# First sweep of a bidirectional recurrent mixer: four passes of 512 tokens, or two of 1024

## The chip, the cores and the metric

The kernel runs on one core of one Trainium2 chip. The metric is device time of one execution in microseconds. Before the change it was 2407.32 us, the median of three runs (2403.57 to 2407.87).

TensorE is called PE in the profile, VectorE DVE, ScalarE ACT, GpSimd POOL and SyncE SP; PEld is TensorE's loading of weights. All transfers are issued from SP's queue.

## The reference

One layer: a bidirectional RG-LRU mixer, then a SwiGLU feed-forward, each with RMS norm, a conditioning shift and scale, and a gated residual. There are T = 2048 latent tokens and 256 context tokens of width D = 1024; the recurrent width is R = 1280, that is NB = 10 columns of 128; the feed-forward is 2816 wide. Cut to what matters:

```python
u = short_conv(h @ w_rec)                       # 4 taps along the tokens, context and latent apart
for d in range(2):                              # forward, backward
    r, i = sigmoid(u @ gate_w[d] + gate_b[d])   # block diagonal, one 128 x 128 block per column n
    log_a = -8 * r * softplus(-lam[d])
    a = exp(log_a); b = sqrt(-expm1(2 * log_a)) * i * u
    h_ctx = scan(a_ctx, b_ctx, 0)               # context first
    h_lat[d] = scan(a_lat, b_lat, h_ctx[-1])    # its last state starts the latent scan
x = x + g1 * ((h_lat[0] + h_lat[1]) * gelu(h @ w_gate)) @ w_out
x = x + g2 * swiglu(norm(x))
```

Products keep nearly full precision: each operand is split into a high part (a cast on ScalarE) and a low part (a subtraction on VectorE), and each product is three matmuls, high x high, high x low, low x high (`mm3`, lines 124 to 126).

## The kernel before, in words

The work is tiled in chunks of C = 512 tokens. **Sweep 1** (`sweep1`, line 561) goes through the four chunks in order of time, the context joined to chunk 0. The tables `ORDER` (line 33) give each pass its order of jobs, for the ten columns n: r(n) is the projection with w_rec and the conv (`rec_unit`, `conv`), g(n) the projection with w_gate (`gate_unit`), z(n) the products of the two directions' gates (`z_unit`). Both weights are read from DRAM and split again in every pass (`unit`, `parts`, lines 99 and 102), and so is gate_w.

The forward scan runs in each pass (`a_tables`, `a_unit`): exp and tanh on ScalarE, square root, then two products and a scan on VectorE (lines 539 to 542), for groups of two to five columns at a time. The backward scan can only start at the end of time. So for chunks 0 to 2 the backward gates go to DRAM (`d_ab`), with the forward states (`d_hf`) and the gate projection (`d_g`); chunk 3, the last pass, scans both directions on chip. Its sum goes to DRAM for six columns (`d_rec`), and `gelus`, `rg_last` take its GELUs and products.

Chunk 2 is brought back while pass 3 runs (`back_some`, `back_units`, `back_load`, `back`): gates, forward states and gate projection are loaded, its tables, backward scan and GELU product run, and `d_rg` is written. Since a pass's conv lacks the two tokens to its right, chunks overlap by two (`halo`, `edge`).

**Sweep 2** (`sweep2`, line 940) takes chunks 3 and 2 together: the output projection of each (`w_out`, tile ps_wo, five pairs of columns read from `d_rg`), the second norm, sums of parts (`combos`), the feed-forward's first product (`up`) with the backward part of chunks 1 and 0 beside it, their output projection, and the second product (`down`).

What the planner decides: the order of instructions on each engine comes from priorities and a simulated timeline; `behind` adds an order within a queue, and `table` keeps all functions of ScalarE that need a table in the order of the program.

Buffers in PSUM: seven single banks under one tag (`bank`, line 129) and one for small sums. In SBUF: rings by tag; `raw` (4) and `op` (6) for weights and other split operands; two rings for the normed activations, so that those of the next chunk can be made while the last ones are read (`norm1_apply`).

Of the kernel before, what the change touches and what calls it, by code (L numbers as in the profile page):

```python
# [12 lines left out]
P = 128  # L13
D = 1024
# [7 lines left out]
NC_ = T // C  # L22
TC = 256
EPS = 1e-6
# [4 lines left out]
RAWS = 4  # L29


KIND = dict(r="rec", g="gate", z="z")
ORDER = (
# [17 lines left out]
class Trunk:  # L51
# [10 lines left out]
    def __init__(self, tc, io):  # L62
        self.tc, self.nc, self.io = tc, tc.nc, io
        self.last_table = self.turn = self.after = None
# [3 lines left out]
    def table(self, ins):  # L68

        if self.last_table is not None:  # L70
            self.behind(ins, self.last_table)
        self.last_table = ins.ins.name
        return ins

    def in_turn(self, ins):

        if self.turn is not None:
            if self.turn:
                self.behind(ins, self.turn)
            self.turn = ins.ins.name  # L80
        return ins
# [10 lines left out]
    def parts(self, raw, name, n=2 * C, eng_h=None, turn=False):  # L92

        nc = self.nc
        t = self.wp.tile([P, 2, n], F32R, tag="op", name=f"op_{name}", bufs=OPS)
        if eng_h == "v":
            nc.vector.tensor_copy(t[:, 0, :], raw)
        else:
            ins = nc.scalar.copy(t[:, 0, :], raw)  # L99
            if turn:  # L100
                self.in_turn(ins)
        nc.vector.tensor_tensor(out=t[:, 1, :], in0=raw, in1=t[:, 0, :].bitcast(F32), op=ALU.subtract)  # L102
        return t
# [88 lines left out]
    def constants_rest(self):  # L192
# [14 lines left out]
        self.edge = cp.tile([P, NB, 3, 2], F32, name="edge")  # L207
# [28 lines left out]
    def mod_first(self):  # L236
# [10 lines left out]
        st = self.te.tile([P, KD, P], F32R, tag="xtok", name="mod_st", bufs=1)  # L247
# [11 lines left out]
    def mod_quarter(self, q):  # L259
        nc, st, sel = self.nc, self.mod_st, self.sel  # L260
        ps = self.bank(f"ps_mod{q}")
        for k in range(KD):
            raw = self.tp.tile([P, C], F32, tag="i", name=f"raw_modf{q}_{k}", bufs=self.ni)
            self.last_mod = nc.sync.dma_start(raw, self.io["mod_f"][q, k]).ins.name
            tags, bufs = (("a", "a"), self.na) if k % 3 == 0 else (("uh", "ul"), self.nu)
            h, l = (self.te.tile([P, C], F32R, tag=tag, name=f"w{s}_modf{q}_{k}", bufs=bufs)
                    for s, tag in zip("hl", tags))
            nc.scalar.copy(h, raw)
            nc.vector.tensor_tensor(out=l, in0=raw, in1=h.bitcast(F32), op=ALU.subtract)
            for w in (h, l):  # L270
                nc.tensor.matmul(ps, st[:, k, :], w, start=(k == 0 and w is h), stop=(k == KD - 1 and w is l))
        rows = self.tp.tile([P, C], F32, tag="g", name=f"mod_rows{q}", bufs=2)
        nc.scalar.copy(rows, ps)
        pc = self.pp.tile([P, C], F32, tag="st", name=f"ps_modc{q}", bufs=1)[:, :8].rearrange("p (i s) -> p i s", s=2)
# [37 lines left out]
    def norm1_load(self, seg, j):  # L312

        t0 = seg * C + j * P
        xt = self.te.tile([P, D], F32, tag="xtok", name=f"xtok{seg}_{j}", bufs=1)
        self.behind(self.nc.sync.dma_start(xt, self.io["x"][t0 : t0 + P]), self.last_raw)
        return xt

    def norm1_stats(self, seg, j, xt):

        nc = self.nc
        n = C // P
        if j == 0:
            self.ss = self.sp.tile([P, n], F32, tag=f"ss{n}", name=f"ss{seg}", bufs=2)
        self.behind(nc.scalar.activation(xt, xt, AF.Square, accum_out=self.ss[:, j : j + 1]), self.last_X)
        return self.rstd_of(self.ss, f"rstd{seg}") if j == n - 1 else None

    def first_loads(self, seg):

        nc = self.nc  # L330
        n = TC if seg < 0 else C
        src = self.io["ctx_t"] if seg < 0 else self.io["x_t"][seg]
        xs = []
        w = C // n
        for k in range(0, KD, w):
            if seg < 0:
                t = self.te.tile([P, w, n], F32, tag="u", name=f"xc{k}", bufs=self.nu)
            else:
                t = self.tp.tile([P, w, n], F32, tag="r", name=f"x0_{k}", bufs=self.nr)
            nc.sync.dma_start(t, src[:, k : k + w, :])  # L340
            xs += [t[:, j, :] for j in range(w)]
        return xs

    def first_stats(self, xs):

        nc = self.nc
        n0 = TC // P
        ps = self.bank("ss_first", n0 + C // P)
        for s, n, c0 in ((-1, TC, 0), (0, C, n0)):
            acc = self.te.tile([P, C], F32, tag="xr", name=f"acc{s}", bufs=3)[:, :n]  # L350
            for k in range(KD):
                sq = acc
                if k:
                    sq = self.tp.tile([P, C], F32, tag="g", name=f"sq{s}_{k}", bufs=2)[:, :n]
                nc.scalar.activation(sq, xs[s][k], AF.Square)
                if k:
                    nc.vector.tensor_tensor(out=acc, in0=acc, in1=sq, op=ALU.add)
            for j in range(n // P):
                nc.tensor.matmul(ps[:, c0 + j : c0 + j + 1], acc[:, j * P : (j + 1) * P], self.ones[:, :1],
                                 start=(c0 == j == 0), stop=(c0 > 0 and j == C // P - 1), skip_group_check=True)  # L360
        y = self.rstd_of(ps, "rstd_first")
        return {-1: y[:, :n0], 0: y[:, n0:]}

    def first_scale(self, xs, bc, after=None):
        for x in xs:
            ins = self.nc.vector.tensor_tensor(out=x, in0=x, in1=bc, op=ALU.mult)
            if after:
                self.behind(ins, after)

    def norm1_apply(self, seg, bc, xs=None, ks=range(KD)):  # L370
        nc = self.nc
        s = 1 if seg < 0 else 0
        n = TC if seg < 0 else C
        out = []
        for k in ks:
            if xs is None:
                xr = self.te.tile([P, C], F32, tag="xr", name=f"xr{seg}_{k}", bufs=3)
                dma = nc.sync.dma_start(xr, self.io["x_t"][seg][:, k, :])
                if self.after:
                    self.behind(dma, self.after)  # L380
            else:
                xr = xs[k]
            a, b = self.A[:, k, s : s + 1], self.B[:, k, s : s + 1]
            if xs is None:
                nc.vector.scalar_tensor_tensor(out=xr, in0=xr, scalar=a, in1=bc, op0=ALU.mult, op1=ALU.mult)
            else:
                nc.vector.tensor_scalar(out=xr, in0=xr, scalar1=a, scalar2=b, op0=ALU.mult, op1=ALU.add)
            if seg < 0:
                hl = self.hp.tile([P, 2, TC], F32R, tag="hx0", name=f"hc{k}", bufs=KD)
                h, l = hl[:, 0, :], hl[:, 1, :]  # L390
            else:
                ring = ("hx1", "hx0", "hx1", "hx1")[seg] if k < KD // 2 else ("hx1", "hx1", "hx0", "hx1")[seg]
                bufs = KD if ring == "hx0" else 2 * KD
                h = self.hp.tile([P, C], F32R, tag=ring, name=f"hh{seg}_{k}", bufs=bufs)
                l = self.hp.tile([P, C], F32R, tag=ring, name=f"hl{seg}_{k}", bufs=bufs)
            if xs is None:
                nc.scalar.activation(h, xr, AF.Identity, bias=b, scale=1.0)  # L397
                nc.vector.scalar_tensor_tensor(  # L398
                    out=l, in0=xr, scalar=b, in1=h.bitcast(F32), op0=ALU.add, op1=ALU.subtract)
            else:  # L400
                nc.scalar.copy(h, xr)
                nc.vector.tensor_tensor(out=l, in0=xr, in1=h.bitcast(F32), op=ALU.subtract)
            out.append((h, l))
        return out

    def slot(self, tag, seg, n, dt=F32):

        if seg >= 0:
# [644 lines left out]
```

## Time and profile before

| | us |
|---|---|
| median of three runs | 2407.32 |
| the profiled execution | 2408.78 |
| its span, first to last instruction | 2407.0 |
| TensorE busy | 2226.5 |
| VectorE busy | 1609.9 |
| ScalarE busy | 1268.0 |

Busy times are of one engine over the whole span. TensorE's clock, as granted, was 0.964 of full speed in the mean. The four passes of sweep 1 begin at 57, 248.4, 397.6 and 544 us, the output projection of chunks 3 and 2 at 746 and the feed-forward's share of the span some 180 us after that.

How to read the rows: a timeline row is start, duration, engine, line, operation and out<-in, with idle time before it in brackets. A group row is line, engine, operation, shapes and count, then busy time and mean nanoseconds of one, then the engine's idle time before them and what ended it. A wait row says which instruction waited for which other one: sum, times, longest.

### The profile page before, as it was taken

To read this page: it belongs to the slowest core of one execution; us is meant where nothing else is said; L and a number is where in the kernel's file an instruction comes from. 1 tells how busy PE (TensorE), PEld (TensorE's weight loads), DVE (VectorE), ACT (ScalarE), POOL (GpSimd) and SP (SyncE) were. 2 spreads that over 40 slices of the span, in tenths; PEclk is the share of its full clock that TensorE was granted. 3 is DMA by queue.
4 is the path that set the end of the run, shared out by engine and by line. 5 is a ranking of instruction groups with operands and counts; after the bars stand their busy time and mean duration, and the time that the engine had idled before them with its cause. 6 is when DMAs were issued, how large, how long until landed. Compare 5 with 4: busy or idle time off the path is not lost.

```text
span 2407.0 us, 27419 instructions
## 1 busy us (share of the span) xinstructions
PE 2226.5 (93%) x9810; PEld 1828.6 (76%) x9810; DVE 1609.9 (67%) x2446; ACT 1268.0 (53%) x1799; POOL 1.6 (0%) x7
## 2 busy tenths in 40 slices
PE   6999899997866785999999999999999999999999
PEld 4888687875754663778777888888888888888887
DVE  8888878887787558666766656874555555544443
ACT  6588776576897533564646444543333333333332
POOL 0000000000000000000000000000000000000000
PEclk8999999998987897999999999999999999999999
DMA  8444567765436764334443478786632222235664
GB/s 282 158 147 171 185 201 245 231 201 166 137 127 215 265 222 131 109 130 165 132 159 128 154 245 277 241 283 229 208 101 79 93 87 84 79 120 199 230 219 151
DMA packets 163721, 420.24 MB, mean 175 GB/s; under 512 B 19200, under 2 KB 26880, under 8 KB 163584
## 3 DMA queue, kind: packets, MB, share of 16 engines
q1 hardware_dynamic: 163584, 418.49, 52.2%
q8 instruction: 76, 1.25, 0.2%
q14 instruction: 61, 0.50, 0.1%
HBM read 333.51 MB, written 84.90 MB: 174 GB/s over the span
## 4 chain that ended last, share of the span: by engine, by line
PE 62%; DVE 14%; ACT 13%; DMA 6%; issue 4%; SPq 0%; DVEq 0%; ACTq 0%
PE ps_dn L124 7%; PE ps_dn L126 7%; PE ps_dn L125 7%; PE ps_be L124 6%; PE ps_be L125 6%; PE ps_be L126 6%; ACT L90 3%; PE ps_ep L126 3%; PE ps_ep L125 3%; PE ps_ep L124 3%; DMA raw_mod<-in_mod_t 2%; PE ps_wo L124 2%; PE ps_wo L125 2%; PE ps_wo L126 2%; ACT r L90 2%
## 5 line engine op out<-in xcount | busy, mean ns | idle before, releaser
L126 PE MATMUL ps_dn<-op_xd,op_wd 128*128 128x512 f32 x704 | 274.7, 390 | 0.0
L125 PE MATMUL ps_dn<-op_xd,op_wd 128*128 128x512 f32 x704 | 273.9, 389 | 0.0
L124 PE MATMUL ps_dn<-op_xd,op_wd 128*128 128x512 f32 x704 | 269.1, 389 | 0.0
L102 DVE TENSOR_TENSOR op_wd<-raw_wd,op_wd 128x1024 fp32r<-128x1024 f32 x88 | 107.7, 1224 | 197.1 <-ACT op_wd L99 197.1
L99 ACT CAST op_wd<-raw_wd 128x1024 fp32r<-128x1024 f32 x88 | 92.7, 1053 | 259.2 <-PE ps_dn L126 210.5
L887 DVE TENSOR_TENSOR s<-ps_ep,s 128x512 f32<-128x512 f32 x88 | 60.7, 690 | 150.9 <-ACT s L912 111.8
L124 PE MATMUL ps_wo<-op_xo,op_wo 128*128 128x512 f32 x320 | 125.3, 408 | 33.6 <-ACT op_xo L99 33.6
L126 PEld LDWEIGHTS ps_dn<-op_xd,op_wd 128*128 128x128 f32 x704 | 132.1, 188 | 28.2 <-issue 0.5
L124 PEld LDWEIGHTS ps_dn<-op_xd,op_wd 128*128 128x128 f32 x704 | 132.1, 188 | 27.6 <-issue 0.5
L125 PEld LDWEIGHTS ps_dn<-op_xd,op_wd 128*128 128x128 f32 x704 | 132.1, 188 | 27.5
L124 PE MATMUL ps_be<-T,op_b 128*128 128x512 f32 x352 | 139.3, 396 | 9.4 <-ACT s L912 9.4
L124 PE MATMUL ps_ep<-T,op_s 128*128 128x512 f32 x352 | 137.3, 391 | 9.3 <-ACT T L827 9.3
L126 PE MATMUL ps_be<-T,op_b 128*128 128x512 f32 x352 | 138.2, 393 | 0.0
L125 PE MATMUL ps_be<-T,op_b 128*128 128x512 f32 x352 | 138.2, 393 | 0.0
L126 PE MATMUL ps_ep<-T,op_s 128*128 128x512 f32 x352 | 137.4, 390 | 0.0
L125 PE MATMUL ps_ep<-T,op_s 128*128 128x512 f32 x352 | 137.4, 390 | 0.0
L912 ACT COPY s<-ps_be 128x512 f32<-128x512 f32 x44 | 25.6, 583 | 205.9 <-PE ps_be L126 205.9
L125 PE MATMUL ps_rec<-hl,op_rec 128*128 128x512 f32 x320 | 127.1, 398 | 4.8 <-DVE hl L398 4.8
L90 ACT ACT_TABLE_LOAD x96 | 123.2, 1283 | 12.5 <-DMA g<-d_g 6.2
L125 PE MATMUL ps_wo<-op_xo,op_wo 128*128 128x512 f32 x320 | 127.8, 400 | 0.9 <-DVE op_xo L102 0.9
L124 PE MATMUL ps_rec<-hh,op_rec 128*128 128x512 f32 x320 | 127.8, 401 | 0.8 <-ACT hh L397 0.5
L126 PE MATMUL ps_wo<-op_xo,op_wo 128*128 128x512 f32 x320 | 127.2, 397 | 0.0
(506 smaller groups left out, 5695.1 us busy)
## 6 DMA issues: line engine op xcount, KB each, us to landing
raw_wd<-in_down SPq DMA_DIRECT2D x88, 512.0 KB, 3.7
raw_xd<-d_act SPq DMA_DIRECT2D x88, 512.0 KB, 4.7
raw_ga<-in_gu SPq DMA_DIRECT2D x44, 512.0 KB, 4.0
raw_gb<-in_gu SPq DMA_DIRECT2D x44, 512.0 KB, 4.2
d_act<-s SPq DMA_DIRECT2D x88, 256.0 KB, 3.5
raw_rec<-in_w_rec SPq DMA_DIRECT2D x40, 512.0 KB, 4.4
raw_gate<-in_w_gate SPq DMA_DIRECT2D x40, 512.0 KB, 3.8
raw_wo<-in_w_out SPq DMA_DIRECT2D x40, 512.0 KB, 4.6
```

Source lines behind the costliest of these rows:

```text
L90: return self.table(self.nc.scalar.activation(out, in_, func, bias=bias, scale=scale))
L99: ins = nc.scalar.copy(t[:, 0, :], raw)
L102: nc.vector.tensor_tensor(out=t[:, 1, :], in0=raw, in1=t[:, 0, :].bitcast(F32), op=ALU.subtract)
L124: ins = mm(ps, w[0], x[0], start=first, stop=False, skip_group_check=shared)
L125: mm(ps, w[0], x[1], start=False, stop=False, skip_group_check=shared)
L126: mm(ps, w[1], x[0], start=False, stop=last, skip_group_check=shared)
L887: v.tensor_tensor(out=t, in0=ps, in1=t, op=ALU.add)
L912: nc.scalar.copy(s3, be)
```

## The change

Sweep 1 has two passes of S = 1024 tokens. Each weight is read and split once per pass. The context is joined to the first pass and gets its own tiles, with two tokens of the second pair appended to it, so that the conv at the end of the first pair has its right neighbour's projection and the overlap of chunks goes.

- PSUM in sweep 1 is three pairs of banks (`pair`) and two single ones (`bank`); in sweep 2 eight single ones. ScalarE and VectorE ops on latent tokens are 1024 wide.
- Each column's scan comes right after its z (`scan_unit`); groups of columns go. In the first pass the forward scan and both context scans run, and `d_g`, `d_hf` and `d_ab` hold the first pair alone.
- In the second pass both directions are scanned on chip. The GELU comes straight from PSUM, and `rg_unit` adds, multiplies and writes `d_rg` for chunks 2 and 3. `d_rec`, `gelus`, `rg_last`, `back_some` and the backward part of chunk 2 go.
- The normed activations of the second pair (`norm1_apply`) go into the same ring of eight as the first pair's. Its sums of squares come from 1024-wide rows in the first pass (`norm1_stats`).
- At the start the sums of squares are made by one-column matmuls for each k, the modulation weights come in transfers of 512 KB through the rings `raw` and `op`, and the second half of the first pair is normed after the first half and the context.
- Modulation rows (`mod_rest`) come two at a time.

```diff
 ORDER = (
-    "r0 r1 g0 r2 z0 g1 r3 z1 r4 z2 g2 r5 g3 z3 r6 z4 r7 z5 g4 r8 g5 z6 g6 r9 z7 g7 g8 g9 z8 z9",
...
+    "r0 r1 z0 g0 r2 z1 g1 r3 z2 g2 r4 z3 g3 r5 z4 g4 r6 z5 g5 r7 z6 g6 r8 z7 g7 r9 g8 g9 z8 z9",
+    "r0 r1 z0 g0 r2 z1 g1 r3 z2 g2 r4 z3 g3 r5 z4 g4 r6 z5 g5 r7 z6 g6 r8 z7 g7 r9 z8 z9 g8 g9",
 )
...
     def bank(self, name, n=C):
-        t = self.pp.tile([P, C], F32, tag="ps", name=name, bufs=7)
+        tag, bufs = ("p1", 2) if self.first else ("ps", 8)
+        t = self.pp.tile([P, C], F32, tag=tag, name=name, bufs=bufs)
...
+    def hx_tiles(self, s):
+        ts = [self.hp.tile([P, 2, S], F32R, tag="hx", name=f"hx{s}_{k}", bufs=KD) for k in range(KD)]
+        return [(t[:, 0, :], t[:, 1, :]) for t in ts]
...
+    def pair(self, name):
+        return self.pp.tile([P, S], F32, tag="p2", name=name, bufs=3)
...
+    def rec_unit(self, s, n, w):
+
+        ps = self.pair(f"ps_rec{s}_{n}")
+        if s == 0:
+            self.project(s, ps, w, (0,))
+            psc = self.bank(f"ps_recc_{n}")[:, :TX]
+            self.project(s, psc, w, ctx=self.hc)
+            self.project(s, ps, w, (1,))
+        else:
+            psc = None
+            self.project(s, ps, w)
...
+            r, i = self.wtile(f"r{s}_{n}_{d}"), self.wtile(f"i{s}_{n}_{d}")
+            for q, dst in ((1, i), (0, r)):
+                ps = self.pair(f"ps_z{s}_{n}_{d}{q}")
+                for h in range(2):
+                    self.mm3(ps[:, h * C : (h + 1) * C], wg[q], part(U["p"], h * C, (h + 1) * C), True, True)
+                self.act(dst, ps, AF.Sigmoid, bias=bias(q))
...
+        for d, a, r, i, st, w in todo:
+            self.act(a, r, AF.Exp, scale=self.c_a[:, d, n : n + 1])
+            self.act(r, r, AF.Tanh, scale=self.c_t[:, d, n : n + 1])
+        for d, a, r, i, st, w in todo:
+            self.act(r, r, AF.Sqrt)
...
+    def rg_unit(self, n):
+
+        nc = self.nc
+        (f, b), g = self.rec.pop(n), self.gel.pop(n)
+        nc.vector.tensor_tensor(out=f, in0=f, in1=b, op=ALU.add)
+        nc.vector.tensor_tensor(out=f, in0=f, in1=g, op=ALU.mult)
+        for q in range(2):
+            nc.sync.dma_start(self.d_rg[2 + q][n // 2][:, n % 2, :], f[:, q * C : (q + 1) * C])
```

## Rows read from the trace of the kernel before

**Rows 1.** The profile page: the span, busy time of each engine.

```profile
span 2407.0 us, 27419 instructions
...
PE 2226.5 (93%) x9810; PEld 1828.6 (76%) x9810; DVE 1609.9 (67%) x2446; ACT 1268.0 (53%) x1799; POOL 1.6 (0%) x7
```

**Rows 2.** Windows: stretch, length, busy (x) of PE, PEld, DVE, ACT, POOL, PEclk, DMA.

```profile
0.00:57.00 57.00, 35.92 (x116) 24.81 (x117) 49.25 (x108) 38.65 (x68) 1.59 (x7) 0.89 0.82 284
57.00:248.40 191.40, 184.80 (x962) 156.78 (x963) 163.66 (x362) 145.47 (x261) 0.00 (x0) 0.99 0.49 163
248.40:397.60 149.20, 141.24 (x605) 114.98 (x604) 122.70 (x225) 101.67 (x160) 0.00 (x0) 0.97 0.65 207
397.60:544.00 146.40, 141.35 (x603) 113.55 (x602) 116.68 (x201) 99.62 (x151) 0.00 (x0) 0.99 0.69 218
544.00:746.00 202.00, 153.77 (x722) 130.47 (x720) 160.06 (x279) 165.61 (x269) 0.00 (x0) 0.86 0.47 152
746.00:913.30 167.30, 123.33 (x491) 98.47 (x490) 105.05 (x155) 77.83 (x92) 0.00 (x0) 0.86 0.67 227
```

**Rows 3.** Timeline of PE: start, duration; matmuls of 512 and of 256 columns.

```profile
600.44 0.39 PE L125 MATMUL ps_rec<-hl,op_rec 128*128 128x512 f32 x1
600.66 0.39 PE L126 MATMUL ps_rec<-hh,op_rec 128*128 128x512 f32 x1
...
604.80 0.28 PE L124 MATMUL ps_z_0t<-uh,op_gw 128*128 128x256 f32 x1
604.91 0.28 PE L125 MATMUL ps_z_0t<-ul,op_gw 128*128 128x256 f32 x1
```

**Rows 4.** Waits of PE from 544 to 746: sum, times, longest.

```profile
PE ps_z L124 <- ACT i L90: 22.8, 3, 13.3
PE ps_z L124 <- ACT uh L461: 10.0, 1, 10.0
PE ps_z L124 <- ACT g L90: 5.7, 1, 5.7
PE ps_z_1t L124 <- DVE u L454: 3.7, 1, 3.7
PE ps_z_0t L124 <- ACT i L90: 3.4, 1, 3.4
```

**Rows 5.** Waits of PE from 746 to 913.3.

```profile
PE ps_wo L124 <- ACT op_xo L99: 33.6, 3, 13.9
```

**Rows 6.** Windows of tile ps_wo alone, its second pair of chunks.

```profile
1380.00:1502.00 122.00, 109.22 (x480) 90.09 (x480) 10.21 (x15) 1.00 0.77 260
```

**Rows 7.** Instruction groups of ACT, 57 to 746: busy, mean ns, idle before.

```profile
L90 ACT ACT_TABLE_LOAD x46 | 59.0, 1283 | 1.7 <-DMA bg<-d_g 0.9
L99 ACT CAST op_gate<-raw_gate 128x1024 fp32r<-128x1024 f32 x38 | 39.9, 1054 | 9.8 <-PE ps_gate L126 3.1 <-DMA raw_gate<-in_w_gate 3.1 <-PE ps_rec L126 2.0
...
L90 ACT ACTIVATE i<-ps_z,c_gate_b 128x512 f32<-128x512 f32 x40 | 27.9, 699 | 1.8 <-PE ps_z L126 1.8
```

**Rows 8.** Instruction groups of DVE, 57 to 746.

```profile
L454 DVE SCALAR_TENSOR_TENSOR u<-ps_rec,c_conv_w,u 128x512 f32<-128x512 f32 x120 | 88.6, 744 | 20.1 <-ACT u L451 19.4
L102 DVE TENSOR_TENSOR op_gate<-raw_gate,op_gate 128x1024 fp32r<-128x1024 f32 x40 | 48.7, 1217 | 4.6 <-ACT op_gate L99 4.5
...
L542 DVE TENSOR_TENSOR_SCAN i<-a,state,r 128x512 f32<-128x512 f32 x20 | 25.3, 1274 | 0.0
...
L542 DVE TENSOR_TENSOR_SCAN ic<-ac,rc 128x256 f32<-128x256 f32 x20 | 13.4, 680 | 0.0
```

**Rows 9.** Timeline of PE: the sums of squares at the start.

```profile
17.20 1.70 PE L359 MATMUL ss_first<-ones,acc 128*128 128x1 f32 x8
```

**Rows 10.** Timeline of PE right after a wait in pass 3.

```profile
549.40 0.63 PE L126 MATMUL ps_rec<-hh,op_rec 128*128 128x512 f32 x1
...
549.83 0.63 PE L124 MATMUL ps_rec<-hh,op_rec 128*128 128x512 f32 x1
```

**Rows 11.** DMA issues on the page: KB each, us to landing.

```profile
raw_wo<-in_w_out SPq DMA_DIRECT2D x40, 512.0 KB, 4.6
```

More of the change, by code (lines that the diff above doesn't have):

```diff
@@ L29 @@
 RAWS = 4
-KIND = dict(r="rec", g="gate", z="z")
+WS = 9
+CW = 11
 ORDER = (
[4 rows of a table removed]
+    "r0 r1 z0 g0 r2 z1 g1 r3 z2 g2 r4 z3 g3 r5 z4 g4 r6 z5 g5 r7 z6 g6 r8 z7 g7 r9 g8 g9 z8 z9",
+    "r0 r1 z0 g0 r2 z1 g1 r3 z2 g2 r4 z3 g3 r5 z4 g4 r6 z5 g5 r7 z6 g6 r8 z7 g7 r9 z8 z9 g8 g9",
 )
@@ L63, in __init__ @@
         self.tc, self.nc, self.io = tc, tc.nc, io
-        self.last_table = self.turn = self.after = None
+        self.last_table = self.after = None
     def table(self, ins):
@@ L72, in table @@
         self.last_table = ins.ins.name
[L73 to L80, printed above, removed]
         return ins
@@ L261, in mod_quarter @@
         ps = self.bank(f"ps_mod{q}")
[L262 to L274, printed above, removed]
+        for j in range(KD // 2):
+            raw = self.raw(self.io["mod_f"][q, j], f"modf{q}_{j}")
+            self.last_mod = self.last_raw
+            hl = self.parts(raw, f"modf{q}_{j}")
+            for k in (2 * j, 2 * j + 1):
+                for w in range(2):
+                    nc.tensor.matmul(ps, st[:, k, :], hl[:, w, (k % 2) * C : (k % 2 + 1) * C],
+                                     start=(k == w == 0), stop=(k == KD - 1 and w == 1))
+        rows = self.tp.tile([P, S], F32, tag="w", name=f"mod_rows{q}", bufs=WS)
+        nc.scalar.copy(rows[:, :C], ps)
+        pc = self.bank(f"ps_modc{q}")[:, :8].rearrange("p (i s) -> p i s", s=2)
         for i in range(4):
@@ L342, in first_loads, with first_stats @@
         return xs
-    def first_stats(self, xs):
+    def first_stats(self, xs, cols, name):
         nc = self.nc
[L347 to L370, printed above, removed]
-        nc = self.nc
[L372 to L404, printed above, removed]
@@ L423, in u_tiles @@
-    def u_tiles(self, seg, n):
-        return (self.slot("u", seg, n), self.slot("uh", seg, n, F32R), self.slot("ul", seg, n, F32R))
-    def rec_unit(self, seg, n, w, hx):
-        nc = self.nc
-        L = TC if seg < 0 else C
-        ps = self.bank(f"ps_rec{seg}_{n}", L)
+        ps = self.bank(f"ss_{name}")[:, : len(cols)]
+        segs = sorted({c[0] for c in cols})
+        for k in range(KD):
+            sq = self.wp.tile([P, 2, S], F32, tag="op", name=f"sq{name}_{k}", bufs=OPS)
+            for s in segs:
+                a = min(c[1] for c in cols if c[0] == s)
+                b = max(c[1] for c in cols if c[0] == s) + P
+                nc.scalar.activation(sq[:, -s, a:b], xs[s][k][:, a:b], AF.Square)
+            for i, (s, t0) in enumerate(cols):
+                nc.tensor.matmul(ps[:, i : i + 1], sq[:, -s, t0 : t0 + P], self.ones[:, :1],
+                                 start=(k == i == 0), stop=(k == KD - 1), skip_group_check=True)
@@ L463, in conv, with u_parts @@
-        start = 0 if seg <= 0 else seg * C - 2
-        return dict(seg=seg, n=n, u=u, uh=uh, ul=ul, w=w_, start=start)
-    def gate_unit(self, seg, n, w, hx, direct=False):
-        nc = self.nc
-        ps = self.bank(f"ps_gate{seg}_{n}")
-        for k in range(KD):
-            ws = slice(k * P, (k + 1) * P)
-            mm = self.mm3(ps, (w[0][:, ws], w[1][:, ws]), hx[k], k == 0, k == KD - 1)
-            if k == 0 and (seg, n) == (0, 0):
-                self.behind(mm, self.mod_done)
-        if direct:
-            g = self.tp.tile([P, C], F32, tag="i", name=f"g{seg}_{n}", bufs=self.ni)
-            self.act(g, ps, AF.Gelu_apprx_tanh)
-            return g
-        g = self.tp.tile([P, C], F32, tag="g", name=f"g{seg}_{n}", bufs=2)
-        nc.scalar.copy(g, ps)
-        nc.sync.dma_start(self.d_g[n][:, seg * C : (seg + 1) * C], g)
+    def u_parts(self, t, u):
+        self.nc.scalar.copy(t[:, 0, :], u)
+        self.nc.vector.tensor_tensor(out=t[:, 1, :], in0=u, in1=t[:, 0, :].bitcast(F32), op=ALU.subtract)
+        return t
@@ new lines, in gate_unit, with wtile @@
+    def gate_unit(self, s, n, w):
+        nc = self.nc
+        ps = self.pair(f"ps_gate{s}_{n}")
+        self.project(s, ps, w)
+        if s == 1:
+            g = self.hp.tile([P, S], F32, tag="hc", name=f"g{s}_{n}", bufs=4)
+            self.act(g, ps, AF.Gelu_apprx_tanh)
+            self.gel[n] = g
+        else:
+            g = self.wtile(f"g{s}_{n}")
+            nc.scalar.copy(g, ps)
+            nc.sync.dma_start(self.d_g[n], g)
+    def wtile(self, name):
+        return self.tp.tile([P, S], F32, tag="w", name=name, bufs=WS)
@@ L508, in z_unit @@
-            for dst, ps, q in parts:
-                self.act(dst, ps, AF.Sigmoid, bias=self.gate_b[:, d, q, n : n + 1])
-            nc.vector.tensor_tensor(out=i, in0=i, in1=U["u"], op=ALU.mult)
-            s0 = U["start"]
-            if d not in U["dirs"]:
-                nc.sync.dma_start(self.d_ab[n][:, 0, s0 : s0 + w], r)
-                nc.sync.dma_start(self.d_ab[n][:, 1, s0 : s0 + w], i)
-            elif d == 1 and seg == NC_ - 1:
-                nc.vector.tensor_copy(self.edge[:, n, 0, :], r[:, 0:2])
-                nc.vector.tensor_copy(self.edge[:, n, 1, :], i[:, 0:2])
@@ L565, in sweep1 @@
-        self.d_hf = [self.dp.tile([P, T], F32, name=f"d_hf{n}") for n in range(NB)]
-        self.d_ab = [self.dp.tile([P, 2, T], F32, name=f"d_ab{n}") for n in range(NB)]
-        self.d_rec = [self.dp.tile([P, C], F32, name=f"d_rec{n}") for n in range(NB)]
+        self.d_g = [self.dp.tile([P, S], F32, name=f"d_g{n}") for n in range(NB)]
+        self.d_hf = [self.dp.tile([P, S], F32, name=f"d_hf{n}") for n in range(NB)]
+        self.d_ab = [self.dp.tile([P, 2, S], F32, name=f"d_ab{n}") for n in range(NB)]
@@ new lines, in sweep1 @@
+                if (p, n) == (0, 1):
+                    self.decay()
+                for _ in range(2 if p == 0 and n else p and 2):
+                    if rest:
+                        self.mod_rest(rest.pop(0))
+                if p == 0 and n >= 2:
+                    y = self.norm1_stats(n - 2)
+            elif kind == "gate":
+                self.gate_unit(p, n, W.pop(job))
+                if p == 0 and n == NB - 1:
+                    self.norm1_apply(y)
+                if p == 1 and n in self.rec:
+                    self.rg_unit(n)
+            else:
+                U = pend.pop(n)
+                gw = self.unit(io["gate_w"][n], f"gw{p}_{n}", whole=True)
+                self.z_unit(U, gw)
+                self.scan_unit(U)
+                if n in self.gel:
+                    self.rg_unit(n)
@@ L704, in back_load @@
-        self.behind(nc.sync.dma_start(t["bg"], self.d_g[n][:, c * C : (c + 1) * C]), self.last_raw)
+        cs = slice(c * C, (c + 1) * C)
+        t = {k: self.tile2("ld", f"{k}{c}_{n}") for k in ("br", "bi", "bh", "bg", "ba")}
+        srcs = (self.d_ab[n][:, 0], self.d_ab[n][:, 1], self.d_hf[n], self.d_g[n])
+        for k, src in zip(("br", "bi", "bh", "bg"), srcs):
+            self.behind(nc.sync.dma_start(t[k], src[:, cs]), self.last_raw)
         return t
@@ L794, in norm2_bc @@
         n = C // P
-        ps = self.pp.tile([P, C], F32, tag="st", name=f"ss_ps{c}", bufs=1)[:, :n]
+        ps = self.bank(f"ss_ps{c}")[:, :n]
         for j in range(n):
```

390 lines of the change are left out of this document (174 added, 216 removed), and 3 rows, old and new, of the table ORDER.

## The prediction

> **What bounds the kernel now.** First the page's totals: TensorE is busy for 93% of the span, VectorE 67%, ScalarE 53% [rows 1]. That says that the matmuls are the frame and nothing about where the time is lost, so the second view is the windows by stage, cut at the starts of the four passes, of the output projection and of the feed-forward [rows 2]. The boundaries are read off TensorE's timeline: a pass begins where its first ps_rec matmul follows the last ps_z of the pass before.
>
> The third view is that timeline itself, for the price of one matmul. At full clock matmuls of 512 columns start some 0.22 us apart (600.44, 600.66) and those of 256 some 0.11 (604.80, 604.91) [rows 3], by two decimals; over longer runs I count 0.2265 and 0.12, and 480 of the first kind were 109.22 us of busy time [rows 6]. The durations printed, 0.39 and 0.28, overlap. Counts come from the code, since a few per cent of the records are missing. Per pass there are 10 columns n, and per n 24 matmuls of ps_rec, 24 of ps_gate and 12 of ps_z. Floors: pass 0 has also 240 + 120 narrow context matmuls, so 600 x 0.2265 + 360 x 0.12 = 179 us; passes 1 and 2 have 600 x 0.2265 = 136 us each; pass 3 has 480 x 0.2265 + 240 x 0.12 = 137.5 us, its ps_z being cut at 258 columns. Together 588 us.
>
> Against them stand 191.4, 149.2, 146.4 and 202.0 us, together 689 [rows 2]: the losses are 12, 13, 10 and 64.5 us, **101 us in all**. Three passes run within 8% of TensorE's floor, with VectorE busy 80 to 86%. The fourth is different: it scans both directions, and at the same time brings the backward part and the GELUs of chunk 2 and 3 back from DRAM. There the waits of TensorE are nearly all those of ps_z, for a PSUM bank that ScalarE has not yet emptied (released by i or g) or for the cast of u, 22.8 + 10.0 + 5.7 + 3.7 + 3.4 = 46 us [rows 4].
>
> The next stage is as bad: the output projection of chunks 3 and 2 is 480 matmuls, 480 x 0.2265 = 109 us, and TensorE was indeed busy for 109.22 us with the same 480 later on [rows 6], but from 746 to 913.3 they took 167.3 us at a clock of 0.86 [rows 2]. 33.6 us of that is ps_wo waiting for op_xo [rows 5], the split activations that only exist once the backward scans of chunk 2 and the late GELUs have run. **Loss 58 us.** After 913.3 comes the tail of norm, combos and feed-forward, 2407.0 - 913.3 = 1493.7 us.
>
> **The change part by part.**
>
> **Matmuls.** The same products, in two passes of 1024 tokens. Pass 0: 10 x (48 + 48 + 24) of 512 and 360 narrow ones, 1200 x 0.2265 + 43 = 315 us. Pass 1: 1200 x 0.2265 = 272 us. Sum 587 against 588: nothing gained here.
>
> **Weights, read and split twice rather than four times.** Forty units of w_rec and w_gate and twenty of gate_w go. One costs 1.054 us on ScalarE [rows 7] and 1.217 us on VectorE [rows 8], gate_w about half: some 52 us of ScalarE, 62 us of VectorE. None of it is on TensorE's path, which is why it isn't counted as a gain; it decides whether the new pass 1 still fits beside the matmuls.
>
> **Pass 1, the work per n beside 60 x 2 x 0.2265 = 27.2 us of matmuls.** Durations at 1024 elements are estimates carried on linearly: a scan is 0.680 at 256 and 1.274 at 512, so 2.46; a plain 1024-wide op is 1.217, and a conv op on PSUM, 0.744 at 512, some 1.26 [rows 8]. A cast is 1.054 at 1024; a sigmoid, 0.699 at 512, some 1.1 [rows 7]. VectorE per n: three conv ops 3.8, the low parts of u and of the weights 1.2 + 1.2 + 1.2 + 0.7, two products with u 2.4, per direction 1.2 + 1.2 + 2.5, sum and product with the GELU 2.4, and two modulation rows in seven of the ten n at 1.2 each: 24.4, less some 0.07 of overlap for each, about 24 us or 88%. ScalarE: casts 2.7 + 1.05, conv 1.2, four sigmoids of some 1.1 each 4.4, four exp/tanh 4.5, two roots 2.1, one GELU 1.1, four table loads 5.1 [rows 7]: 22 us or 81%. Both fit, barely; pass 3 of before had 80% and 82% [rows 2] and lost a third. In pass 0 the context is added but only one latent direction is scanned: some 23 and 24 us beside 31.5 us.
>
> **PSUM in pairs.** This is the added wait. Before there were seven single banks; now there are three pairs and two singles. ps_z of one n needs four pairs one after the other, and one of the three is still held by ps_rec of the next n until its conv is through (1.2 on ScalarE, 3.8 on VectorE). So pairs C and D of ps_z wait until ScalarE has loaded the sigmoid table and emptied A and B: A is full at 1.36 us, the load ends at 2.7, the sigmoids of A and B at 3.7 and 4.8, so D can begin at 5 and ends at 6.5 where 5.4 is the floor: **1.1 us per n at the least**. Queued behind it on TensorE are the gate of this n and the rec of the next, so nothing refills the gap. If ScalarE is inside a weight cast or waits for the conv on its way, more is lost; pass 3, the nearest rows of this kind, lost the 46 us of [rows 4] for ten n, 4.6 us each. I take 2.4 us, nearer to the low end, because the new order puts one scan between two ps_z and not two or three, and no chunk-2 tables are mixed in: 20 x 2.4 = **48 us** (22 to 92).
>
> **Start.** The squares' sums move from VectorE to TensorE: 56 + 32 one-column matmuls in place of 6. Four took 1.70 us at low clock, 0.43 each [rows 9], so 24 us at most for the first set, beside DMA-bound loading of the modulation weights in 57 us of which TensorE used 36 [rows 2]. Then the second half of the first pair must be normed before rec 0 can end: eight times scale, apply, subtract of some 1.7 us on VectorE. Rec 0 and rec 1 of the first half and their context, 2 x 8.3 us of matmuls, run meanwhile. I put **8 us** (0 to 20).
>
> **Turn of the passes.** The normed activations of the second pair go into the same eight buffers as the first, so each waits for the last use by gate 9. Behind it ScalarE and VectorE take some 1.1 us for each of eight, at the pace at which gate 9 frees them (1.4 us), and ps_z 8 and 9 lie in between; the same scans fall due then. **10 us** (0 to 20), up to the whole of eight times 2.4 us. The turns of before went through other buffers and are no measure.
>
> **Rest of the sweep**: what passes 1 and 2 lost, 13 and 10 us for 136, came from modulation rows awaited from DRAM and conv chains; these are half as many and twice as long. **15 us** (5 to 25).
>
> **Between the sweeps.** The whole backward part of chunk 2, its loads, its tables and the late GELUs go. After gate 9: a table load, GELU, product, store to d_rg and load back, some 14 us with a DMA at the 4.6 us of [rows 11] each way, which only the fifth of five input pairs needs; the first four are 96 matmuls, 22 us. It is covered; if it were not, the old 33.6 us stand for it. I put **8 us** (0 to 35) for the projection. The DRAM traffic of d_rec, and of chunks 2 and 3 in d_g, d_hf and d_ab, goes with it, and was hidden.
>
> **Unchanged**: from 913.3 on. One bank tag with eight buffers in place of seven and one gives ss_ps a bank of the ring; taken as zero, since the banks are as many as before.
>
> **Sum**, against the profiled span: 57 + 587 + (48 + 8 + 10 + 15) + 109 + 8 + 1493.7 = 2335.7, for 2407.0 before. The profiled execution took 2408.78, 1.8 around its span and 1.5 above the median of 2407.32. So about **2336 us, 71 us less**.
>
> [...] The table loads are 46 in sweep 1 [rows 7], and each n now has its own scan: 3 x 10 + 4 x 10 = 70. A load is 1.283 us by the row, and so is counted above. [...]
>
> **The rivals.**
> - **Pairs cost only their floor** (1.1 us per n) and the turn and start are covered: 22 + 18 lost in place of 89. 2336 - 49 = 2287. For it: passes 0 to 2 lost only 7 to 10%. Chance 0.17.
> - **A convoy at ps_z: slower than before.** The sigmoid that frees a pair stands behind a cast of u that itself waits for VectorE's conv; single waits of 10.0 and 13.3 us occurred before [rows 4]. At 8 us per n it costs 160 in place of 48: 2448. It decides from 2.4 + 71/20 = 5.9 us per n. [...] Against it: VectorE and ScalarE are below 90%. Chance 0.10. [...]
> - [...] Chance 0.05.
> - **The hole between the sweeps stays**, 33.6 us of waits for op_xo by another cause (loads of 1 MB per 5.4 us, or the switch of pools): 2336 + 34 = 2370. Chance 0.08.
> - My forecast, 2310 to 2365: 0.60.
>
> **How the numbers follow.** 0.2% is 5 us, what a measurement can tell. Faster: all but the convoy and a slice of the upper bounds, 0.87; same 0.03; slower 0.10. The range takes in the low rival and the upper cases of the hole and of the tables with 4 us per n: 2285 to 2395; the convoy is left out.
>
> **What would show it.** Right: ps_wo begins near 725 and its 480 matmuls take under 125 us; TensorE's waits are ps_z on ScalarE, some 2 to 3 us per n; table loads near 70. Wrong: ps_wo beginning after 760, waits of ps_z above 6 us, a pass 1 with ScalarE above 95%, or a start whose first rec ends after 90 us.

## The result, and the profile after

The changed kernel takes 2502.17 us in the median (2498.40 to 2503.88), the kernel before, timed beside it, 2405.95: a ratio of 1.040 with an interval of 1.038 to 1.0416. It is slower by 96 us where 71 us less were forecast.

The page of the changed kernel, beside [rows 1]:

```profile
span 2496.6 us, 26085 instructions
...
PE 2274.3 (91%) x9854; PEld 1868.5 (75%) x9854; DVE 1529.7 (61%) x2007; ACT 1192.7 (48%) x1445; POOL 1.6 (0%) x7
```

VectorE and ScalarE lost 80 and 75 us of work, more than the 62 and 52 put down for the weights that are no longer split again; what made the rest was not looked into. TensorE has the same products and 48 us more busy time, 16 of it ahead of rec 0, where the one-column sums are; its granted clock was 0.948 in the mean, against 0.964. Windows by stage, as [rows 2] (start; rec 0 and 1 up to the first z; pass 0 to the end of gate 7; the turn, that is r9 to z9; pass 1; the projection):

```profile
0.00:62.20 62.20, 52.23 (x197) 43.17 (x198) 36.38 (x79) 31.14 (x44) 1.60 (x7) 0.92 0.66 224
62.20:124.15 61.95, 48.46 (x231) 41.14 (x229) 51.55 (x134) 25.54 (x45) 0.00 (x0) 0.78 0.17 62
124.15:429.70 305.55, 256.35 (x1185) 215.25 (x1185) 177.69 (x283) 180.31 (x234) 0.00 (x0) 0.92 0.36 129
429.70:500.93 71.23, 54.96 (x238) 44.28 (x237) 51.20 (x70) 40.05 (x51) 0.00 (x0) 0.87 0.45 166
500.93:875.60 374.67, 298.73 (x1202) 241.52 (x1200) 247.75 (x233) 227.32 (x214) 0.00 (x0) 0.87 0.21 72
875.60:998.50 122.90, 113.53 (x489) 93.07 (x488) 72.36 (x91) 49.55 (x57) 0.00 (x0) 0.94 0.65 225
```

No engine is full in either pass: VectorE has 58 and 66% of the third and the fifth stretch, ScalarE 59 and 61%. The projection begins at 875.6 and not at 746, and then goes in 123 us with no wait for op_xo, against the 167.3 of before. So the hole between the sweeps is closed, and the loss lies in sweep 1. TensorE's waits from 60 to 876 say where, as [rows 4] did for pass 3:

```profile
PE ps_z L112 <- ACT op_gw L89: 65.6, 9, 10.4
PE ps_zc L112 <- ACT op_gw L89: 58.5, 8, 9.3
PE ps_z L112 <- ACT i L83: 26.0, 3, 11.8
...
```

17 of the 20 z units wait for **op_gw**, the cast of gate_w, 124.1 us in all. Before, no wait for it is among those of [rows 4]. ScalarE's timeline around one of these waits (start, duration, line, operation, idle time before and what ended it):

```profile
564.40 1.20 ACT L427 ACTIVATE u<-ps_rec,c_conv_b,c_conv_w 128x1024 f32<-128x1024 f32 x1 [9.10 <-PE ps_rec L114]
569.65 1.04 ACT L433 CAST uhl<-u 128x1024 fp32r<-128x1024 f32 x1 [4.05 <-DVE u L430]
570.60 0.61 ACT L89 CAST op_gw<-raw_gw 128x512 fp32r<-128x512 f32 x1
571.12 1.04 ACT L89 CAST op_rec<-raw_rec 128x1024 fp32r<-128x1024 f32 x1
...
```

and TensorE's, just behind the wait:

```profile
571.27 0.80 PE L112 MATMUL ps_z<-uhl,op_gw 128*128 128x512 f32 x1 [6.91 <-ACT op_gw L89]
571.86 0.63 PE L113 MATMUL ps_z<-uhl,op_gw 128*128 128x512 f32 x1
572.29 0.63 PE L112 MATMUL ps_z<-uhl,op_gw 128*128 128x512 f32 x1
...
574.33 0.40 PE L112 MATMUL ps_z<-uhl,op_gw 128*128 128x512 f32 x1
574.56 0.39 PE L113 MATMUL ps_z<-uhl,op_gw 128*128 128x512 f32 x1
```

Read together: rec n+1 ends at about 564.4. ScalarE, idle for 9.10 us, makes the conv's first step, then stands 4.05 us at the cast of u of **n+1**, which needs VectorE's three conv steps; only behind it comes op_gw of **n**, for which z of n has been waiting on TensorE since rec n+1 ended. TensorE waits for a chain that belongs to the next column. The transfers that feed op_gw had landed long before; the tile raw_gw from 520 to 575:

```profile
L96 SPq DMA_DIRECT2D raw_gw<-in_gate_w x2: 327/328/328, 534.7 to 550.1; - x2
...
DMA to landing us min/median/max: 2.7/2.7/2.7
```

Both had landed by 552.8. ScalarE did not take op_gw out of its order all the same: it stood idle for 9.10 and 4.05 us, 13 in all, with op_gw's input there.

The first eight matmuls behind the wait take 3.29 us from start to start where 8 x 0.2265 would be 1.81, another 1.5 us. They go with the granted clock: it was 1.00 from 550 to 564, ahead of the 6.91 us of idleness, 0.52 from 571.27 to 574.33, where matmuls start 0.43 us apart, and 1.00 again from 574.33 to 580. In [rows 10] they stand as far apart, and the granted clock was 0.50 there (549.40 to 552.00). The next z begins 35.75 us later, at 607.02; the floor is 27.2. From z to z in pass 1 it is 35.75 to 37.27 us: the wait, and 1.7 to 3.2 us more.

### The profile page after: what moved, and what is told of

It reads as the page before. It is cut to its first block, busy times and chain, and to the rows that moved or that the text cites. A ratio compares the mean times of both kernels' runs of the same rounds, so it can differ in the third digit from the quotient of the medians.

```text
span 2496.6 us, 26085 instructions
## 1 busy us (share of the span) xinstructions
PE 2274.3 (91%) x9854; PEld 1868.5 (75%) x9854; DVE 1529.7 (61%) x2007; ACT 1192.7 (48%) x1445; POOL 1.6 (0%) x7
## 4 chain that ended last, share of the span: by engine, by line
PE 78%; ACT 9%; DVE 8%; issue 3%; DMA 3%; ACTq 0%; SPq 0%; DVEq 0%
PE ps_dn L114 6%; PE ps_dn L113 6%; PE ps_dn L112 6%; PE ps_be L112 6%; PE ps_be L113 5%; PE ps_be L114 5%; DVE u L430 3%; PE ps_ep L113 3%; PE ps_ep L114 3%; PE ps_ep L112 3%; PE ps_rec L113 3%; PE ps_rec L114 3%; PE ps_rec L112 3%; PE ps_gate L112 3%; PE ps_gate L113 3%
## 5 line engine op out<-in xcount | busy, mean ns | idle before, releaser
L112 PE MATMUL ps_z<-uhl,op_gw 128*128 128x512 f32 x160 | 81.6, 510 | 92.2 <-ACT op_gw L89 65.6
L113 PE MATMUL ps_rec<-hx,op_rec 128*128 128x512 f32 x320 | 126.7, 396 | 3.0 <-DVE hx L363 3.0
L112 PE MATMUL ps_rec<-hx,op_rec 128*128 128x512 f32 x320 | 126.4, 396 | 1.2 <-ACT hx L362 1.2
L114 PE MATMUL ps_rec<-hx,op_rec 128*128 128x512 f32 x320 | 126.0, 394 | 0.0
L112 PE MATMUL ps_gate<-hx,op_gate 128*128 128x512 f32 x320 | 125.2, 391 | 0.0
L112 PE MATMUL ps_wo<-op_xo,op_wo 128*128 128x512 f32 x320 | 125.0, 394 | 0.0
```

Of the source, the lines that this page charges most:

```text
L112: ins = mm(ps, w[0], x[0], start=first, stop=False, skip_group_check=shared)
L113: mm(ps, w[0], x[1], start=False, stop=False, skip_group_check=shared)
L114: mm(ps, w[1], x[0], start=False, stop=last, skip_group_check=shared)
```

## Experiments

The theories: **A**, the place of op_gw on ScalarE costs the time, and it stands there because u's split now takes its buffers from the ring op, which gate_w uses too; **B**, the three pairs of PSUM banks cost it; **C**, the start does. **S** is a rival to A: the ring's size itself.

**gate_w gets a buffer of its own (gw_own_slot).**

```diff
 def parts(self, raw, name, n=2 * C):
...
+    if name.startswith("gw"):
+        t = self.te.tile([P, 2, n], F32R, tag="gw", name=f"op_{name}", bufs=1)
+    else:
         t = self.wp.tile([P, 2, n], F32R, tag="op", name=f"op_{name}", bufs=OPS)
```

> The changed kernel, but gate_w's split operand has a buffer of its own (one of 4 KB per partition) and no longer takes one of the six in the ring op. Theory A: the 124 us for which ps_z waits for the cast op_gw are a place in ScalarE's queue (the cast stands behind the cast of u, which waits for VectorE's conv), and it stands there because the ring op has no free buffer earlier. Then the wait nearly goes (under 15 us), with some 1.5 us of low clock behind each of the 17: 2502 - 124 - 25 = 2353 (2335 to 2385). Rival B: PSUM pairs bind. ps_z needs pairs that rec holds until its conv is done, so the wait only changes its name to the sigmoids i and r: within 25 us of 2502.

Measured: 2367.67 us (2366.54 to 2368.82), 0.985 of before (0.9835 to 0.9865), 134 us below the changed kernel. TensorE's waits from 60 to 876, then the windows from the first z of pass 0 into gate 9, from there to rec 0 of pass 1, and pass 1:

```profile
PE ps_z L115 <- ACT i L83: 27.4, 12, 7.0
...
PE ps_z L115 <- ACT uhl L436: 5.5, 2, 5.1
```

```profile
121.83:399.80 277.97, 277.71 (x1324) 229.84 (x1325) 196.83 (x312) 189.80 (x246) 0.00 (x0) 0.99 0.43 148
399.80:442.23 42.43, 25.40 (x98) 19.25 (x97) 32.11 (x43) 31.76 (x39) 0.00 (x0) 0.79 0.53 190
442.23:745.63 303.40, 282.53 (x1201) 226.90 (x1200) 242.62 (x232) 224.92 (x213) 0.00 (x0) 0.98 0.27 88
```

From the first z to gate 9 of pass 0 TensorE never stands still, with the same pairs of banks: B falls as the cause of the 96 us. ScalarE now casts op_gw between two sigmoids of the z before, and u's cast finds its conv done:

```profile
502.02 0.62 ACT L92 CAST op_gw<-raw_gw 128x512 fp32r<-128x512 f32 x1 [0.28 <-PE ps_z L117]
502.54 1.11 ACT L83 ACTIVATE r<-ps_z,c_gate_b 128x1024 f32<-128x1024 f32 x1
...
504.97 1.15 ACT L83 ACTIVATE a<-r,c_a 128x1024 f32<-128x1024 f32 x1
506.02 1.03 ACT L436 CAST uhl<-u 128x1024 fp32r<-128x1024 f32 x1
```

**The same buffer, the old place (own_slot_old_order).** A buffer and an order were changed at once; this takes back the order alone.

```diff
+    ins = nc.scalar.copy(t[:, 0, :], raw)
+    if name.startswith("gw"):
+        self.behind(ins, self.last_uh)   # the latest cast of u
...
 def u_parts(self, t, u):
-    self.nc.scalar.copy(t[:, 0, :], u)
+    self.last_uh = self.nc.scalar.copy(t[:, 0, :], u).ins.name
```

> gate_w keeps its own buffer as in gw_own_slot (2367.67 us), but the planner is made to put the cast op_gw of n on ScalarE behind the cast uhl of n+1, where the changed kernel has it. Theory A (it is the place in ScalarE's order that costs; the ring of six only caused it): the waits of ps_z and ps_zc for op_gw come back, some 7 us for each n, and the time is 2480 to 2510. Rival S (the room in the ring is what helps, weights and u's split being earlier there): the time stays under 2400.

Measured: 2502.76 us (2501.62 to 2505.04), the time of the changed kernel, and its waits; ScalarE's rows below show its order:

```profile
PE ps_z L117 <- ACT op_gw L92: 63.0, 10, 6.9
PE ps_zc L117 <- ACT op_gw L92: 59.9, 9, 9.3
```

```profile
572.13 1.04 ACT L438 CAST uhl<-u 128x1024 fp32r<-128x1024 f32 x1 [4.04 <-DVE u L435]
573.08 0.61 ACT L92 CAST op_gw<-raw_gw 128x512 fp32r<-128x512 f32 x1
```

One cast of 0.61 us, put behind the cast of u in ScalarE's order, costs 135 us. So A stands in what it says of the place.

**One buffer less in the ring (own_slot_five_buffers).** OPS = 5, and gate_w keeps its own.

> gate_w has its own buffer, and the ring op for everything else has five buffers in place of six, less room in all than the changed kernel has. Theory A (the order counts, and with a buffer of its own gate_w's cast stays ahead of u's): 2360 to 2390, no wait for op_gw in steady state. Rival S (the number of buffers counts): waits for op_rec, op_gate or uhl appear in both passes, over 2430.

Measured: 2390.88 us (2386.68 to 2394.32). One wait for op_gw is left, of 1.4 us, as in gw_own_slot; ps_wo begins at 751.4 against 745.6, and the first ps_be at 894.1 against 889.2, so most of the 23 us lie behind it, where the feed-forward uses the ring too. S falls: with less room in all than the changed kernel has, it is 111 us faster. It is a little over its range, since the expectation left sweep 2 out.

**gate_w's split one job earlier, in the old ring (gw_one_job_earlier).** In the loop over jobs `unit(gate_w)` is called ahead of the job before z.

> The changed kernel, but gate_w of a z is loaded and split one job earlier in the program, ahead of the rec (or gate) that precedes the z; all rings as they are. Theory A: the place in the queue alone decides, so the wait of ps_z for op_gw goes: 2353 (2335 to 2390), unless the ring op is so short that the casts of w_rec and w_gate come late in its place, which would show as waits of ps_rec or ps_gate for op_rec and op_gate. Rival B (PSUM pairs): within 25 us of 2502.

Measured: 2391.76 us in one run, just over the upper end. Waits for op_gw are down to 11.9 us; 14.0 us for rc and 33.1 for i are left. So most of the loss goes with the six buffers as they are, if gate_w is asked for early enough; 24 us above gw_own_slot remain.

**z behind the gate (z_behind_gate).** ORDER of both passes: r0 r1 g0 z0 r2 g1 z1 ... r9 g8 z8 g9 z9.

> The changed kernel with another order of jobs in both passes: r0 r1 g0 z0 r2 g1 z1 ... so that a gate's 11 us of matmuls lie between a rec and the z that follows; rings as they are. Theory A: the conv, the cast of u and op_gw fall beside the gate, and ps_z finds its operand: some 120 us of the waits go, but the last z of pass 0 stands alone before the turn: 2370 (2345 to 2400). Rival B (PSUM pairs): the conv of the rec is also through by then and gives its pair back, so B expects a gain here too, some 100 us; the run tells A and B only from the view that slow conv arithmetic itself is the bound (no gain).

Measured: 2447.92 us in one run, a miss: the gain is 54 us, where A and B alike had expected 100 or more. Waits for op_gw of 43.3 + 26.3 us remain although a gate stands between, for op_gw still stands behind the cast of u, now behind op_rec as well, and ScalarE waits there for VectorE:

```profile
567.29 1.04 ACT L433 CAST uhl<-u 128x1024 fp32r<-128x1024 f32 x1 [12.57 <-DVE u L430]
568.24 1.04 ACT L89 CAST op_rec<-raw_rec 128x1024 fp32r<-128x1024 f32 x1
569.19 0.61 ACT L89 CAST op_gw<-raw_gw 128x512 fp32r<-128x512 f32 x1
```

**u's cast on VectorE (u_cast_on_vector).**

```diff
 def u_parts(self, t, u):
-    self.nc.scalar.copy(t[:, 0, :], u)
+    self.nc.vector.tensor_copy(t[:, 0, :], u)
```

> The changed kernel (2502 us) with one line changed: the cast of u to its high part is made on VectorE, behind the conv that it waits for, and no longer on ScalarE. gate_w stays in the ring op. Theory A (ScalarE stands at that cast, and op_gw stands behind it): op_gw can be cast while VectorE still has the conv, the waits for op_gw fall from some 7 us for each n to under 3, and the time is 2380 to 2440, less gain than gw_own_slot since the cast lengthens VectorE's chain to z by some 1.2 us for each n. Rival (the ring's six buffers hold gate_w back whoever casts u): 2470 to 2510.

Measured: 2456.63 us (2454.45 to 2460.57), between the two expectations. TensorE's waits:

```profile
PE ps_z L112 <- DVE u L430: 25.3, 9, 6.6
PE ps_zc L112 <- DVE u L451: 19.7, 9, 4.1
PE ps_z L112 <- ACT op_gw L89: 16.2, 9, 1.8
PE ps_zc L112 <- ACT op_gw L89: 12.6, 7, 1.8
...
PE ps_z L114 <- DVE op_gw L90: 1.1, 1, 1.1
```

The waits for op_gw fell from 124.1 to 28.8 us in all, none above 1.8, as A has it. Of what is left, 45.0 us are for the conv steps of L430 and L451, the last ones that read ps_rec and the context's bank ps_recc. They aren't for the low part of op_gw, which VectorE also makes behind the conv: that is 1.1 us. What would explain them is that z needs a PSUM tile that rec n+1 still holds, which is B's mechanism; no run takes that apart. In gw_own_slot, with the same banks, such a wait is seen once, at the first z (4.0 us).

**The start (start_sums_on_vector, own_slot_start).** The squares are added up on VectorE, and 7 and 4 one-column matmuls stay of 56 and 32; the first on the changed kernel, the second on gw_own_slot.

> The changed kernel, but at the start the squares are added up on VectorE over k, as before the change, and only the last sums go through one-column matmuls (7 and 4 in place of 56 and 32). Theory C: these matmuls cost the start, since the modulation matmuls begin at 32.7 us behind them where they began at 15.4 before, and 10 us of the second set lie between rec 0 and the rest: 12 to 22 us less, 2484. Rival: the start is bound by the transfers and by VectorE's norming, so that nothing changes (within 5 us).

> gate_w has its own buffer, and the squares at the start are summed on VectorE again, as in start_sums_on_vector, which brought the first z 8 us forward and the end not at all. Theory C (the start was swallowed by the convoy of pass 0 only): without the convoy the 8 us come through, 2357 to 2363. Rival: something else sets the pace of pass 0 (VectorE's work on the context and the weights, or the loads), 2365 to 2370.

Measured: 2498.46 us (2497.22 to 2503.99) and 2365.85 us (2361.60 to 2366.44). The first z came 8.3 and 4.7 us earlier, the end at most 4 and 2 us: C falls as the cause of the 96 us, and the second expectation goes to its rival.

**The ends of the passes (own_slot_ends).** ORDER ends with r9 z8 g8 g9 z9 and with r9 z8 g8 z9 g9.

> gate_w has its own buffer, and the ends of the passes are r9 z8 g8 g9 z9 (first) and r9 z8 g8 z9 g9 (second) in place of g8 g9 z8 z9 and z8 z9 g8 g9, so that z8 and z9 no longer stand back to back. In gw_own_slot the two ends show 17 and 12 us of waits of TensorE for i, r and u's split. If these come from two z in a row: 8 to 20 us fewer, 2348 to 2360. Rival: the turn is set by VectorE and ScalarE norming the second pair and the end by the last scans, so that the wait only moves to ps_rec of the next pass and to ps_wo: 2363 to 2373.

Measured: 2356.71 us (2356.01 to 2357.52), 11 us less, as expected for two z no longer back to back. Pass 1 begins 16 us earlier, and then z0 waits 9.71 us for a conv that VectorE starts only at 451.65, behind the last of the second pair's norm, two modulation rows and z9's scans.

**What stands in the start's queues (ends_rows_behind, ends_rows_sums).** The chain of waits of gw_own_slot, where the second half of the first pair is to be normed (start, duration):

```profile
78.42 4.35 DMA raw_mod<-in_mod_t
...
84.12 3.50 DMA raw_mod<-in_mod_t
...
88.91 3.68 DMA xtok<-in_x
92.69 1.15 ACT xtok L310 x2
93.84 0.48 ACT bcn L157
```

Three transfers that nothing needs yet stand ahead of the norm. ends_rows_behind orders their uses behind it (`self.behind(ins, self.scale1)` for the first four rows, `self.behind(ins, self.bc1_done)` for the token row); ends_rows_sums also has the sums on VectorE.

> own_slot_ends (2356.71 us) with one thing more: the first four modulation rows' products on VectorE are ordered behind the scaling of the first pair's second half, and the first token row's squares on ScalarE behind the copy of its norm. In own_slot the chain to the first z shows 4.35 + 3.50 us of VectorE waiting for those rows' DMAs and 3.68 + 1.15 us of ScalarE with the token row, between the end of the sums of squares (82 us) and the scaling (94.35), while the norm itself takes some 4 us. Theory (a transfer that nothing needs yet stands ahead of the norm in two queues): the first z comes 7 to 11 us earlier, near 112, and the time is 2346 to 2352. Rival (the second half's conv waits for VectorE's other work anyway, or the gain is swallowed in pass 0 as in own_slot_start, where 4.7 us earlier gave 2): 2353 to 2358.

> ends_rows_behind and the squares at the start summed on VectorE again. Theory (the 32 + 56 one-column matmuls at low clock cost TensorE's order in the start, and what they cost comes through once the norm is no longer held up): 3 to 8 us below ends_rows_behind. Rival (VectorE's eight additions more per set take what TensorE gives): within 3 us of ends_rows_behind.

Measured: 2359.29 us (2358.61 to 2360.24), a miss by its rival's side and beyond, and 2353.31 us (2351.02 to 2355.37). The chain of ends_rows_behind:

```profile
68.80 10.88 PE ss_b L344 x64
...
90.51 0.87 PE n_bc L151 x2
...
107.63 3.65 DMA raw_mod<-in_mod_t
...
112.57 3.53 DMA xtok<-in_x
```

Two things had hidden behind the first. TensorE's own order holds the norm's matmul n_bc until rec 0's first half is through at 90.4, which itself stood behind 10.88 us of one-column sums; and the rows' transfers now stand ahead of the conv. With the sums on VectorE n_bc starts at 82.4 and the first z at 117.5, 7.3 us earlier, and now 6 us of it reach the end. Whether the rows' order has a share in that isn't shown: own_slot_ends with the sums alone was not run. **ends_rows_sums** is the fastest version found: 0.979 of before (0.9774 to 0.9807).

**z9 behind the next pass's rec 0 (late_z9_rows).** On ends_rows_behind, with `jobs` changed so that z9 of pass 0 follows rec 0 of pass 1. The edit has a second part, which its expectation doesn't name: the whole of pass 0 takes the order of z_behind_gate (r0 r1 g0 z0 r2 g1 z1 ...).

> ends_rows_behind, but z9 of the first pass stands behind rec 0 of the second pass, so that the conv of rec 0 has z9's matmuls beside it (in own_slot_ends z0 of the second pass waited 9.71 us for VectorE's conv, and z9 5.18 us for i). Theory (two short jobs between two long ones): 5 to 12 us below ends_rows_behind. Rival (rec 0 now waits for the norm of the second pair, since only g9 frees its buffers and nothing stands between): equal or up to 8 us above.

Measured: 2387.89 us (2385.76 to 2393.42), 29 us slower, worse than the rival. Rec 0 did wait 6.76 us for hx. But 18.8 us of new waits lie in pass 0, where ps_z waits six times for u and eight times for the copy of ps_gate, and there the order of jobs was another. With two changes in one run, what z9's place is worth isn't shown.

## Why the prediction was wrong

The sum, against what the two kernels show. The projection is counted up to 19.75 us ahead of the first ps_be, as 913.3 lies before (933.05), and the matmuls of sweep 1 are the forecast's 587 for both kernels:

| us | forecast | changed | gw_own_slot |
|---|---|---|---|
| up to the first z, less 27.5 of matmuls | 57 + 8 = 65 | 124.15 - 27.5 = 96.6 | 94.3 |
| pass 0 beyond its matmuls | | 376.8 - 287.5 = 89.3 | 32.9 |
| pass 1 beyond its matmuls | | 374.7 - 272 = 102.7 | 31.4 |
| both (pairs 48, turn 10, rest 15) | 73 | 192.0 | 64.3 |
| matmuls of sweep 1 | 587 | 587 | 587 |
| projection | 117 | 121.8 | 123.8 |
| what follows | 1493.7 | 1499.2 | 1496.5 |
| span | 2335.7 | 2496.6 | 2365.9 |

- **The step that failed is "PSUM in pairs"**, where z's waits were priced. It asked when a bank is free, and never when z's other operand, op_gw, is cast. The change has it in one line (454 of the changed kernel): u's split moved into the ring op, beside the weights and gate_w. In what order ScalarE would then make the four casts was not asked, and the planner makes that order anew. 119 of the 161 us between forecast and span are here (192 - 73); with op_gw ahead of u's cast, in gw_own_slot, the 192 fall to 64.3.
- **The convoy** was there as a rival at 0.10 and 2448 us. It named the cast of u that waits for VectorE's conv, and this is the cast at which ScalarE stood. It had the wrong thing behind it (the sigmoid that frees a pair, not op_gw), and its point of decision was passed: 17 waits of 7.3 us, and slow matmuls behind each (in the 2.85 to 4.98 us right behind a wait the granted clock was 0.50 to 0.52, each time). Against it stood that VectorE and ScalarE are below 90%; at some 60% they waited for each other all the same, because order and not load made the wait. What stands ahead of the matmuls of [rows 10], 0.43 us apart, is no wait for a bank either, but one of 1.86 us for an operand's low part:

```profile
549.03 0.58 PE L125 MATMUL ps_rec<-hl,op_rec 128*128 128x512 f32 x1 [1.86 <-DVE hl L398]
```

- **The pairs themselves** were over-priced: in gw_own_slot z waits 0.93 us for i in pass 1 and the period is 28.66 us, 1.5 above the floor where 2.4 were taken. In pass 0, up to gate 9, no wait is seen behind the first z.
- **The turn** was 10 (0 to 20). In gw_own_slot the 42.43 us from 399.80 on hold some 19 us of matmuls, so it lost about 24. (The other 9 of the 32.9 lie before, where TensorE is busy throughout: some 3 go to the first 5.5 us, at whose end matmuls of 512 columns start 0.43 us apart, from 124.73 to 126.86, and the rest was not looked into.) Of its two long waits the first, 5.58 us, is the convoy once more. The sigmoid of z8 stands behind two casts of the second pair's norm, and these wait for VectorE. It waits 1.17 us for the first row's transfer, and then takes 2.7 us for each of the eight buffers (1.41 for the scalings, 1.28 for the subtraction, from 413.35) where some 1.1 were taken:

```profile
412.93 1.15 ACT L387 ACTIVATE hx<-xr,B_mix 128x1024 fp32r<-128x1024 f32 x1 [2.72 <-DVE xr L386]
...
415.99 1.11 ACT L83 ACTIVATE i<-ps_z,c_gate_b 128x1024 f32<-128x1024 f32 x1
```

  In the second, 7.02 us, the sigmoid of z9 stands behind z8's tables and three more casts of the norm. The end of pass 1 wasn't priced at all and costs some 12 (waits of 5.12 and 6.74 us); it too has two z in a row, and own_slot_ends, which parts them, gained 11 us at both places together. That the 64.3 lie near the forecast's 73 is luck: these two errors made up for the pairs.
- **The start** was 8 (0 to 20) and is 39.6, or 37 with the convoy gone. The first set of one-column sums was priced, at 24 us at most, and took 23.89 from 8.97 on; a low clock was named for it, but from 10 to 34 the granted clock was 1.00, so its pace isn't shown to be the clock's. The second set was left to stand beside rec 0; it lies in TensorE's order inside it, the norm lies behind the row transfers, and the conv of rec 0 behind both.
- **Right**: the matmuls, the work for each column in pass 1 (24.8 us of VectorE and 22.7 of ScalarE, by the windows of the changed kernel, for 24 and 22), the projection (121.8 for 117; the waits of [rows 5] are gone, so the hole closed), and that table loads don't make ScalarE the bound. They are 70, as counted:

```profile
L83 ACT ACT_TABLE_LOAD x70 | 89.8, 1283 | 1.3
```

  The range took in a case in which the tables cost more than their loads of 1.283 us. No run shows such a cost: the 70 loads have 1.3 us of idle time before them in all, and the operation behind one starts 1.30 us after the load's start (532.33, 533.63 in gw_own_slot).

Three of the four signs of being wrong came: ps_wo at 875.6, waits of 7.3 us at ps_z, and a rec 0 whose second half only begins at 98.2. One reading was off without weight: passes 0 to 2 of the kernel before lay 7, 10 and 8% above their floors, so not all three within 8%.

What stays open: why the planner, given one buffer more, puts op_gw ahead. That the shared ring has a part in it follows from gw_own_slot and own_slot_five_buffers, and gw_one_job_earlier shows that in the same ring an earlier request nearly does; but the choice itself wasn't looked into. Open too is what holds z for VectorE's conv in u_cast_on_vector.

## What to carry to other kernels

When an edit moves a tile into a ring that other operands use, ask of each operand of the waiting matmul where its cast will stand in its engine's order, and what the instruction ahead of it waits for; VectorE and ScalarE, busy for 58 to 66% of the two passes here, gave no cover against that. A wait that is taken away at the head of a queue shows what stood behind it, so the gain of such an edit is bounded by the next wait and not by the removed one. And if one edit changes both room and order, put the old order back alone: that told the two apart in one run.

## What had not been expected of the hardware

A pause of 0.93 us left TensorE's matmuls 0.23 us apart right behind it (499.25, 499.49 in gw_own_slot), one of 6.91 us brought five at 0.43 in a row (571.86 to 574.00 in the changed kernel), and the others of that length in pass 1 up to thirteen; the granted clock was 0.50 to 0.52 behind them. And the cast of u, 128 x 1024, took 0.69 us on VectorE (617.90 in u_cast_on_vector) against 1.04 on ScalarE, where the expectation had taken 1.2, the time of a subtraction of that size.
